# Row loads of the experts and input-tile loads issued from GpSimd's queue

## The chip, the cores and the metric

The kernel runs on one core of a Trainium2 chip. The metric is the device time of one execution in microseconds (us). Before the change it is 1392.5 us (median of 3 runs, 1391.55 to 1395.13).

A core has TensorE (PE in the profile, its weight loads PEld), VectorE (DVE), ScalarE (ACT), GpSimd (POOL) and SyncE (SP). Each executes its own instructions in order. A load between device memory and the core's own memory is issued by an instruction of SP, ACT or POOL (SPq, ACTq, POOLq in the profile, where POOL's part of the work also shows on POOL itself) and is carried out by 16 DMA engines that all queues share. Semaphores tell when it has landed.

## The reference

One decoder layer over 1024 tokens of 1024 numbers, in f32:

```python
h = rms_norm(x, attn_norm_g);  x = x + parallel_mixer(h, ...)          # two attentions, gated
h = rms_norm(x, mem_x_norm_g); x = x + memory_cross_attention(h, mem)  # 256 memory rows
h = rms_norm(x, moe_norm_g);   x = x + hierarchical_moe(h, ...)
# in the mixer: proj = h @ w_in; keys and queries are normalised and rotated (rope) by position
# in the moe:   each token picks one of 4 groups, then 2 of its 4 experts; 16 experts in all
y = y + combine[..., e] * ((silu(h @ w_gate[e]) * (h @ w_up[e])) @ w_down[e])
```

Each expert has three f32 matrices, gate and up of 1024x256 and down of 256x1024.

## The kernel before, in words

Products are made at nearly f32 accuracy: an operand is split into a high and a low part (ACT copies to the high part, DVE or POOL subtracts), and three matmuls are summed (`mm3`, L530 to L532). A planner fixes the order of the instructions on each engine when the kernel is built. It takes them by the order in which the program states them and by its own estimate of when each could start; `tc.issue_after(q)` puts what follows behind instruction `q` where both are on one engine. A tile pool with `bufs=n` has n buffers in turn, and a write to a buffer waits for the last reader of what it held.

**The start (`prep`, L733).** Eight tiles of 128 tokens of `x` go through the same steps. `load_x` (L794) loads one into one of three buffers; `square_x` (L819) sums its squares on ACT; `newton` (L546 to L552) makes the reciprocal root on DVE in 12 small instructions; L830 scales the tile with the row `grow`; PE transposes it (L608) and ACT and DVE split it into `hT`; and `project` (L530 to L532) multiplies it with 360 columns of `w_in`. These columns come in four blocks of three loads each (`kraw`, L805) and are split on ACT (L839) and on DVE and POOL in turn (L840). SP issues x tile 0, block 0, block 1, tile 1, block 2, block 3, tile 2; tiles 3 to 7 are issued by POOL as buffers come free. `table_inputs` (L663) issues seven small loads on ACT's queue: positions, frequencies, `grow`, and the four gain rows `g_k`, `g_mk`, `g_q`, `g_mq`; the gains are wanted only by `tables` (L672), which writes the tables of sines and cosines to device memory (`d_tab`), from which each tile reads its part two steps later. The first ACT instruction after them is a small activation on `ident` (L821) that loads ACT's function table.

**The experts (`moe`, L1655).** Tokens have been scattered by expert into a table `d_xs` in device memory, 1032 numbers a row, by 16 indirect DMAs of POOL (L197, `route.puts`): the vector and, behind it, its weights and token number. The experts are taken in an order by their counts, read at run time from `nb` into registers of SP (`values_load`, L1669, L1848), as SP's loads of weights and rows take their addresses from these.

- `rows_in` (L1675) loads the rows of expert number k: one DMA for each 128 rows into `xg` (two buffers, `xg_[k % 2]`, L1682) and one for their tails into `emore` (L1687). Each waits for all scatters and for the last reader of the buffer. The first 128 rows of the first two experts are loaded early (`early`), before the scatter of the second half of the tokens.
- `rows_of` (`tokens`, L1692) makes the token numbers `etok` and weights `ewt` from `emore` on DVE (L1706 to L1711), transposes the rows on PE (L1718) and splits them.
- `gate_up_in` loads gate and up in two halves of two DMAs each into `gu_raw` (L1733, two buffers); `gate_up` splits them (ACT L1747, DVE L1748). `down` loads and splits the down matrix (`dn_raw`, L1756 to L1759).
- `first_small` or `first_big` and `second` do the matmuls; ACT scales the product into `ey` (L1780, four buffers), and POOL adds it to the output by token number with an accumulating indirect DMA (`result`, L1765). Each of these waits for the one before it, as both touch the output.

Iteration i of the loop over the experts states, in this order: rows of expert i+2 (`load`), half of the gate and up weights of i+1 and its tokens, the first product of i, the other half of i+1, the down matrix of i, and the second product and result of i-1. Row loads and weight loads are all on SP's queue, in this order. Large experts (two blocks of rows) and small ones (one) alternate.

Of the kernel before, what the change touches and what calls it, by code (L numbers as in the profile page):

```python
# [498 lines left out]
class Hybrid:  # L499
# [163 lines left out]
    def table_inputs(self, pool, xp):  # L663
        nc, I = self.nc, self.I
        pi = pool.tile([128, T], I32, name="pos_i")
        p = I['positions']
        nc.scalar.dma_start(pi, bass.AP(tensor=p.tensor, offset=p.offset, ap=[[1, 128], [128, T]]))
        inv = self.row('inv_freq', 0, 32, "inv", pool, nc.scalar)
        grow = self.row('attn_norm_g', 0, D, "grow", xp, nc.scalar)
        return grow, [pi, inv] + [self.row(*a, pool, nc.scalar) for a in (('dsa_k_norm_g', 0, 64, "g_k"), ('mla_k_norm_g', 64, 32, "g_mk"), ('dsa_q_norm_g', 0, 64, "g_q"), ('mla_q_norm_g', 64, 32, "g_mq"))]  # L670

    def tables(self, pool, inputs):  # L672
        nc, I = self.nc, self.I
# [58 lines left out]
    def prep(self):  # L732
        tc, nc, I = self.tc, self.nc, self.I  # L733
        V, A, G = nc.vector, nc.scalar, nc.gpsimd
# [12 lines left out]
        tk = lambda t: slice(t * 128, (t + 1) * 128)  # L747

        def chunk(cols, pool=None, dve=False):
            n = sum(b - a for a, b in cols)  # L750
            per = 512 // n
            ws = []
            for k0 in range(0, KD, per):
                srcs, o = [], 0
                for k in range(k0, k0 + per):
                    for a, b in cols:
                        srcs.append((W[k * 128:(k + 1) * 128, a:b], o))
                        o += b - a
                hi, lo = self.wpiece(srcs, o, pool=pool, dve=dve)
                for i in range(per):  # L760
                    ws.append((hi[:, i * n:(i + 1) * n], lo[:, i * n:(i + 1) * n]))
            return ws, n
# [29 lines left out]
        xt = {}  # L792

        def load_x(t):  # L794
            xt[t] = xp.tile([128, D], F32, name="xt", bufs=3)
            (nc.sync if t < 3 else nc.gpsimd).dma_start(xt[t], I['x'][0, tk(t), :])

        c3 = ExitStack()
        load_x(0)

        kcols, kraw = ((512, 640), (1152, 1224), (1480, 1640)), []
        for h, (pool, nm) in enumerate(((kp, "kvb"), (hp, "ik_hi"), (kp, "kvb"), (hp, "ik_lo"))):
            raw, o = pool.tile([128, S], F32, name=nm)[:, 0:720].rearrange("p (k n) -> p k n", k=2), 0
            for a, b in kcols:
                nc.sync.dma_start(raw[:, :, o:o + b - a], W[h * 256:h * 256 + 256, a:b].rearrange("(k p) n -> p k n", p=128))  # L805
                o += b - a
            kraw.append(raw)
            if h % 2:
                load_x(1 + h // 2)
        tp_ = c3.enter_context(tc.tile_pool(name="tb", bufs=1, side="right"))  # L810
        grow, tin = self.table_inputs(tp_, xp)
        ckv_row = self.row('mla_ckv_norm_g', 0, 128, "ckv_row", hp)
        cq_row = self.row('mla_cq_norm_g', 0, 256, "cq_row", hp)
        ms = Stats()
        ev, st2, cTs, kvb = {}, {}, {}, {}
        xj = xp.tile([128, D], BF16, name="xj", bufs=1)

# [5 lines left out]
        for i in range(T + 7):  # L823
# [4 lines left out]
            if i < T:  # L828
                xn = xp.tile([128, D], F32, name="xn", bufs=2)
                last_xn = V.scalar_tensor_tensor(xn, xt[i], y[:, 0:1], grow, op0=OP.mult, op1=OP.mult)  # L830
                rows_T = self.transpose_rows(xn, hT[0][:, :, tk(i)], hT[1][:, :, tk(i)])
                if 2 < i + 2 < T:
                    load_x(i + 2)
            if i == 0:
                ws, n = [], 360
# [12 lines left out]
            t = i - 1  # L848
# [9 lines left out]
            t = i - 3  # L858
            if 0 <= t < T:
# [20 lines left out]
                p = self.tp()  # L880
# [9 lines left out]
            t = i - 4  # L890
# [12 lines left out]
            t = i - 6  # L903
# [15 lines left out]
        ws, n = chunk([(640, 1152)], dve=True)  # L919
        off, o = {}, 0  # L920
# [7 lines left out]
        for i in range(2, T + 2):  # L928
            if i < T:
                ev[i] = project(ws, n, i)  # L930
            t = i - 1
# [12 lines left out]
            t = i - 2  # L944
# [32 lines left out]
        ms = self.sm.tile([128, 17], F32, name="ms")  # L977
# [9 lines left out]
        for cols, o in (((1224, 1480), 0), ((0, 512), 256)):  # L987
            ws, n = chunk([cols], (self.wraw, up) if o == 0 else None)
            for t in range(T):

                at = -20 + 8 * t if o == 0 else 20 + 3 * t
# [662 lines left out]
    def moe(self, route):  # L1654
        tc, nc, I = self.tc, self.nc, self.I  # L1655
        V, G, A = nc.vector, nc.gpsimd, nc.scalar
        tk = lambda t: slice(t * 128, (t + 1) * 128)
        SP = [mybir.EngineType.SP]
        c = ExitStack()


# [4 lines left out]
        rt = route.rt  # L1666
        r1.tile([128, 8 * T], F32, name="spare")
        nb = route.nb
        lead = [nc.values_load(nb[0:1, i:i + 1], engines=SP, min_val=0, max_val=NE - 1) for i in range(2)]  # L1669
        flat = lambda p, nm, dt=F32: p.tile([128, 2048], dt, name=nm)  # L1670
        table = self.d_xs.rearrange("(e r) f -> e r f", e=NE)

# [2 lines left out]
        def rows_in(n, ex, r, xg, early=False):  # L1675


            at = slice(ex, ex + 1) if isinstance(ex, int) else ds(ex, 1)
            loads = []
            for b in range(0, n, 128):  # L1680
                m = min(128, n - b)
                last_load = nc.sync.dma_start(xg[0:m, b // 128], table[at, r + b:r + b + m, 0:D].rearrange("o p f -> (o p) f"))  # L1682
                loads.append(last_load)
            more = rt.tile([128, 2, 4], F32, name="emore", bufs=4)
            for b in range(0, n, 128):
                m = min(128, n - b)
                loads.append(nc.sync.dma_start(more[0:m, b // 128], table[at, r + b:r + b + m, D:D + 4].rearrange("o p f -> (o p) f")))  # L1687
            for q in loads:
                for p in route.puts:
                    if early and p in route.late:  # L1690
                        tc.declare_no_dep(q.ins, p.ins, reason="rows of a later block")
                    else:  # L1692
                        tc.add_manual_dep(q.ins, p.ins.name, mybir.DependencyInfo(mybir.DependencyClass.Sync, mybir.DependencyReason.DATA), reason="rows of the table")
            return n, xg, more, last_load
# [73 lines left out]
        ends, count = [None] * 4, [0]  # L1768
# [55 lines left out]
        xg3 = lambda t: t.rearrange("p (b f) -> p b f", f=D)  # L1824

        def early(i, ex, exf):

            a = (r3 if i else ra).tile([128, D], F32, name="ey" if i else "dn_raw", bufs=2)
            h, l = (eT[i][0][:, z * 1024:z * 1024 + 1024] for z in range(2))
            return rows_of(rows_in(128, ex, 0, xg3(a), True), exf, [cut(w, 128) for w in (h, l)], True)  # L1830
# [6 lines left out]
        xg_ = [flat(r1, f"xg{i}") for i in range(2)]  # L1837

        expert, loaded = [0, lead[0], lead[1]], {}

        def load(k):
            if k < NE:
                n, r = (ROOM[k] - 128, 128) if k < 2 else (ROOM[ORDER_[k]], 0)
                if k > 2:
                    with tc.issue_after(loaded[k - 1][3].ins):
                        expert.append(nc.values_load(nb[0:1, 16 + ORDER_[k]:17 + ORDER_[k]], engines=SP, min_val=0, max_val=NE - 1))  # L1848
                loaded[k] = rows_in(n, expert[k], r, xg3(xg_[k % 2]))

        def tokens(k):
            n, exf = loaded[k][0], (0.0, route.le[:, 0:1])[k] if k < 2 else route.ex[:, ORDER_[k]:ORDER_[k] + 1]
            return n, rows_of(loaded[k], exf, [cut(w, n) for w in eT[k % 2]])
# [4 lines left out]
        nb = route.places(r3)  # L1858
        raws = [gate_up_in(2, expert[2], h) for h in range(2)]
        load(0)  # L1860
        load(1)
        nA, h = tokens(0)
        last = (128, rest(), dn, *hA[2:])
        rest = first_small(128, gu1, hB)
        second(*last)
        hA = h
        load(2)
        nB, h = tokens(1)
        last = (128, rest(), dn1, *hB[2:])
# [6 lines left out]
        n, hT = tokens(2)  # L1876
# [4 lines left out]
        for i in range(2, NE):  # L1881
# [10 lines left out]
            if i + 1 < NE:  # L1892
                n, hT = n1, hT1
# [4 lines left out]
        with ExitStack() as c:  # L1898
# [5 lines left out]
            with tc.If(nov > 0):  # L1904
# [7 lines left out]
                for a, b, room in runs:  # L1912
                    r = room // 128
                    with tc.For_i(a, b, 1) as s_:
                        ne = nc.values_load(nb[0:1, ds(s_ + 32, 1)], min_val=0, max_val=9 - r)
                        ex = nc.values_load(nb[0:1, ds(s_ + 16, 1)], min_val=0, max_val=NE - 1)
                        with tc.For_i(0, ne, 1) as k:
                            ix, it, iw = op.tile([128, 1], I32, name="oix"), op.tile([128, 1], I32, name="oit"), op.tile([128, 1], F32, name="oiw")
                            at, f, num = op.tile([128, 2], F32, name="oat"), op.tile([128, 4], F32, name="of"), route.cnt[:, ds(ex, 1)]
# [18 lines left out]
                            for h in range(2):  # L1938
                                p = self.tp().rearrange("p (a b) -> p a b", a=4)
# [56 lines left out]
```

## Time and profile before

| | |
|---|---|
| median of 3 runs | 1392.5 us |
| profiled execution, whole | 1393.33 us |
| its span (first to last instruction) | 1391.6 us |
| PE busy | 1237.9 us |
| DVE, ACT, POOL busy | 949.3, 806.8, 440.1 us |
| read from and written to device memory | 134.61 and 69.70 MB |

The start is the stretch from 0 to about 60 us; the experts are from about 1085 us to the end. A group of rows of the timeline has the start in us, the duration in us, the engine, the line and operation, and in brackets the idle time before with what ended it. A window's row has its length, then the busy us of PE, PEld, DVE, ACT and POOL with their counts, the granted TensorE clock as a share of full speed, the busy share of the DMA engines and their rate in GB/s.

### The profile page before, as it was taken

Reading aid. Unit: us, or ns where it says so; the run is one execution under the profiler, and the core shown is the slowest. Engines: PE = TensorE matmul, PEld = TensorE weight load, DVE = VectorE, ACT = ScalarE, POOL = GpSimd, SP = SyncE. Lnnn points to the kernel's source line nnn. Section 1 sums busy time; section 2 is a strip of 40 time slices with the busy share of each in tenths; the row PEclk is TensorE's granted clock in tenths of the full one; section 3 lists DMA queues with packets and bytes.
Section 4 is the critical chain, followed back from the end, with each engine's and each line's share of the span. In section 5 each row is a group of like instructions: output and inputs, shape, how many; then the busy total and the mean of one; then the engine's idle time right before and its main releaser. Section 6 shows DMA issues by size and latency. Waiting matters only on the chain.

```text
span 1391.6 us, 20751 instructions
## 1 busy us (share of the span) xinstructions
PE 1237.9 (89%) x6884; PEld 1036.9 (75%) x6885; DVE 949.3 (68%) x1967; ACT 806.8 (58%) x1667; POOL 440.1 (32%) x537
## 2 busy tenths in 40 slices
PE   3998999998899999999988999999999378999983
PEld 2877778777687788887777787887888266887772
DVE  6886956799999477878977466133367735677661
ACT  4654656887662488889988322034365335676652
POOL 4565100648774322121343221121133431021111
PEclk9999999999899999999999999998999689999997
DMA  7565003543426545445221233531022757899972
GB/s 207 159 199 148 12 24 101 163 131 123 136 102 188 153 130 182 142 166 166 63 84 46 80 127 121 199 86 39 31 77 76 282 216 233 271 342 295 289 224 37
DMA packets 145557, 203.54 MB, mean 146 GB/s; under 512 B 69632, under 2 KB 90880, under 8 KB 145440
## 3 DMA queue, kind: packets, MB, share of 16 engines
q1 hardware_dynamic: 134944, 172.57, 38.4%
q0 software_dynamic: 7440, 24.71, 6.6%
q10 hardware_dynamic: 3056, 4.84, 0.9%
q8 instruction: 56, 0.92, 0.3%
q14 instruction: 61, 0.50, 0.1%
HBM read 134.61 MB, written 69.70 MB: 147 GB/s over the span
## 4 chain that ended last, share of the span: by engine, by line
PE 48%; DVE 19%; ACT 12%; DMA 11%; issue 6%; POOL 2%; SPq 1%; DVEq 0%; ACTq 0%; POOLq 0%
PE acc L530 5%; PE acc L531 5%; PE acc L532 5%; PE s L530 4%; PE s L531 4%; PE s L532 4%; DMA gu_raw<-in_moe_w_gate_dram 2%; ACT tk_junka L1222 2%; PE tp L1378 2%; PE s L955 2%; DVE ik_hi L1212 1%; PE tp L1475 1%; DVE ik_lo L1212 1%; PE acc L1392 1%; PE acc L1391 1%
## 5 line engine op out<-in xcount | busy, mean ns | idle before, releaser
L522 POOL TENSOR_TENSOR wl<-wr,wh 128x512 fp32r<-128x512 f32 (+1 forms) x78 | 102.2, 1328 | 164.1 <-ACT wh L521 120.4
L517 DVE TENSOR_TENSOR PT_lo<-tp,PT_hi 128x512 fp32r<-128x512 f32 x152 | 101.7, 685 | 28.2 <-ACT PT_hi L516 27.1
L530 PE MATMUL s<-hT_hi,wh 128*128 128x512 f32 x256 | 103.2, 403 | 3.8 <-ACT s L1083 3.8
L1765 POOL DMA_INDIRECT out_dram<-ey,etok x24 | 39.9, 1661 | 205.7 <-ACT ey L1780 42.9
L532 PE MATMUL s<-hT_hi,wl 128*128 128x512 f32 x256 | 102.3, 402 | 1.6 <-POOL wl L522 1.6
L531 PE MATMUL s<-hT_lo,wh 128*128 128x512 f32 x256 | 102.0, 401 | 0.0
L1748 DVE TENSOR_TENSOR gu_lo<-gu_raw,gu_hi 128x1024 fp32r<-128x1024 f32 x60 | 71.9, 1221 | 40.4 <-ACT gu_hi L1747 40.1
L516 ACT ACTIVATE PT_hi<-tp 128x512 fp32r<-128x512 f32 x152 | 86.8, 594 | 21.5 <-PE tp L1475 9.6
L1222 ACT ACTIVATE tk_junka<-sc,tk_b 128x512 bf16<-128x512 f32 (+2 forms) x96 | 79.4, 827 | 28.0 <-DVE tk_b L1219 27.0
L1747 ACT ACTIVATE gu_hi<-gu_raw 128x1024 fp32r<-128x1024 f32 x60 | 62.2, 1056 | 47.5 <-DMA gu_raw<-in_moe_w_gate_dram 21.6
L521 ACT ACTIVATE wh<-wr 128x512 fp32r<-128x512 f32 (+1 forms) x78 | 47.0, 619 | 73.2 <-PE acc L532 27.8
L532 PE MATMUL acc<-wh,hT_lo 128*128 128x512 f32 (+2 forms) x240 | 85.4, 356 | 0.3 <-DVE hT_lo L517 0.3
L530 PE MATMUL acc<-wh,hT_hi 128*128 128x512 f32 (+2 forms) x240 | 85.2, 356 | 0.2 <-ACT hT_hi L516 0.2
L531 PE MATMUL acc<-wl,hT_hi 128*128 128x512 f32 (+2 forms) x240 | 84.2, 352 | 0.0
L1360 DVE TENSOR_REDUCE low<-s 128x1 f32<-128x256 f32 (+3 forms) x64 | 49.1, 769 | 33.1 <-PE s L1359 32.9
L530 PEld LDWEIGHTS s<-hT_hi,wh 128*128 128x128 f32 x256 | 49.9, 195 | 14.3 <-ACT s L1083 4.5
L530 PE MATMUL s<-eT1h,gu_hi 128*128 128x224 f32 (+2 forms) x192 | 54.1, 282 | 6.9 <-DVE ewt L1711 3.6
L532 PEld LDWEIGHTS s<-hT_hi,wl 128*128 128x128 f32 x256 | 49.7, 194 | 12.0 <-POOL wl L522 2.1
L964 DVE SCALAR_TENSOR_TENSOR sc<-rel,iw,sc 128x384 f32<-128x384 f32 (+5 forms) x42 | 43.3, 1030 | 21.2 <-ACT rel L958 18.0
L531 PEld LDWEIGHTS s<-hT_lo,wh 128*128 128x128 f32 x256 | 49.7, 194 | 10.2
L530 PE MATMUL acc<-wh,mg_hi 128*128 128x512 f32 x128 | 52.4, 415 | 3.1 <-issue 3.1
L531 PE MATMUL s<-eT1l,gu_hi 128*128 128x224 f32 (+2 forms) x192 | 54.5, 284 | 0.0
(552 smaller groups left out, 4140.4 us busy)
## 6 DMA issues: line engine op xcount, KB each, us to landing
d_xs<-zero SPq DMA_DIRECT2D x32, 516.0 KB, 3.6
dn_raw<-in_moe_w_down_dram SPq DMA_DIRECT2D x32, 512.0 KB, 8.5
gu_raw<-in_moe_w_gate_dram SPq DMA_DIRECT2D x30, 512.0 KB, 7.1
gu_raw<-in_moe_w_up_dram SPq DMA_DIRECT2D x30, 512.0 KB, 8.0
wr<-in_w_in_dram SPq DMA_DIRECT2D x48, 256.0 KB, 3.1
d_g<-s SPq DMA_DIRECT2D x32, 256.0 KB, 2.4
gt<-d_g SPq DMA_DIRECT2D x16, 512.0 KB, 3.8
xg<-d_xs SPq DMA_DIRECT2D x13, 512.0 KB, 5.6
```

The lines of the kernel that those rows point to most:

```text
L516: q = self.nc.scalar.activation(hi, src, AF.Copy)
L517: self.nc.vector.tensor_sub(lo, src, hi.bitcast(F32))
L521: self.nc.scalar.activation(hi, src, AF.Copy)
L522: self.nc.gpsimd.tensor_sub(lo, src, hi.bitcast(F32))
L530: mm(out, a[0], b[0], start=start, stop=False)
L531: mm(out, a[0], b[1], start=False, stop=False)
L532: mm(out, a[1], b[0], start=False, stop=stop)
L964: last_sc = V.scalar_tensor_tensor(scv, rel[:, :Wd], g, scv, op0=OP.mult, op1=OP.add)
L1222: A.activation(junka[:, :(t + 1) * 128], blk(t), AF.Sign, bias=b[:, i:i + 1].bitcast(F32), accum_out=cnt[:, i:i + 1])
L1360: nc.vector.tensor_reduce(low[:, b:b + 1], sp[:, 0:nch, 0:w], AX.XY, OP.min)
L1747: A.activation(hi[:, z], raw_z, AF.Copy)
L1748: E.tensor_sub(lo[:, z], raw_z, hi[:, z].bitcast(F32))
```

## The change

At the start, the loads of x tiles 1 to 7 are issued by POOL (before: 3 to 7), tiles 1 and 2 now behind blocks 0 and 1 in the program's order, and the four gain rows are issued by POOL and not by ACT. Two small clears of `ms` are stated ahead of the loads. With the experts, all row loads but the early ones are issued by POOL; POOL reads the numbers of the experts into its own registers for that, and SP reads its numbers behind the last load of a down matrix (`ends[2]`) and not behind a row load.

```diff
-        return grow, [pi, inv] + [self.row(*a, pool, nc.scalar) for a in (('dsa_k_norm_g', ...), ...)]
+        return grow, [pi, inv] + [self.row(*a, pool, nc.gpsimd) for a in (('dsa_k_norm_g', ...), ...)]
...
-            (nc.sync if t < 3 else nc.gpsimd).dma_start(xt[t], I['x'][0, tk(t), :])
+            (nc.gpsimd if t else nc.sync).dma_start(xt[t], I['x'][0, tk(t), :])
+        ms = Stats()
+        ms(0), ms(1)
         load_x(0)
...
-            if h % 2:
-                load_x(1 + h // 2)
+            if h < 2:
+                load_x(1 + h)
...
+            Q = nc.sync if early else G
-                last_load = nc.sync.dma_start(xg[0:m, b // 128], table[...])
+                last_load = Q.dma_start(xg[0:m, b // 128], table[...])
-                loads.append(nc.sync.dma_start(more[0:m, b // 128], table[...]))
+                loads.append(Q.dma_start(more[0:m, b // 128], table[...]))
...
-        expert, loaded = [0, lead[0], lead[1]], {}
+        expert, loaded, row_of = [0, lead[0], lead[1]], {}, [0]
         def load(k):
             if k < NE:
                 n, r = ...
+                if k:
+                    with tc.issue_after(loaded[k - 1][3].ins):
+                        row_of.append(number(k - 1 if k < 3 else 16 + ORDER_[k], POOL))
                 if k > 2:
-                    with tc.issue_after(loaded[k - 1][3].ins):
-                        expert.append(nc.values_load(nb[0:1, ...], engines=SP, ...))
-                loaded[k] = rows_in(n, expert[k], r, xg3(xg_[k % 2]))
+                    with tc.issue_after(ends[2].ins):
+                        expert.append(number(16 + ORDER_[k], SP))
+                loaded[k] = rows_in(n, row_of[k], r, xg3(xg_[k % 2]))
```

## Rows read from the trace of the kernel before

**Rows 1.** The page, busy time of each engine.

```profile
PE 1237.9 (89%) x6884; PEld 1036.9 (75%) x6885; DVE 949.3 (68%) x1967; ACT 806.8 (58%) x1667; POOL 440.1 (32%) x537
```

**Rows 2.** The timeline of the first 17 us, every engine.

```profile
2.37 0.45 ACTq L512 DMA_DIRECT2D g_k<-in_dsa_k_norm_g_dram  x1
...
8.39 1.28 ACT L821 ACT_TABLE_LOAD   x1 [8.27 <-DMA g_q<-in_dsa_q_norm_g_dram]
...
10.09 1.06 ACT L819 ACTIVATE xj<-xt 128x1024 bf16<-128x1024 f32 x1
...
11.28 0.17 DVE L546 TENSOR_SCALAR ms<-ms 128x11 f32<-128x11 f32 x1 [9.49 <-ACT xj L819]
...
16.95 1.97 DVE L830 SCALAR_TENSOR_TENSOR xn<-xt,rq_y,grow 128x1024 f32<-128x1024 f32 x1
```

**Rows 3.** Waits of SP's queue, 0 to 60 us: us in total, times, longest.

```profile
SPq L805 <- DMA pos_i<-in_positions_dram: 2.7, 1, 2.7
```

**Rows 4.** Windows of the start: busy us, clock, DMA share, GB/s.

```profile
20.00:25.00 5.00, 4.95 (x19) 4.25 (x18) 5.00 (x18) 3.56 (x7) 2.56 (x3) 1.00 0.50 159
...
60.00:90.00 30.00, 28.03 (x155) 24.11 (x154) 28.11 (x86) 19.86 (x64) 17.21 (x40) 1.00 0.57 165
```

**Rows 5.** Issues of x tiles by queue: count, min/median/max ns of one.

```profile
L796 POOL DMA_DIRECT2D xt<-in_x_dram x5: 546/582/787, 19.2 to 50.0; - x5
```

**Rows 6.** SP's waits for PE from 1080 us on; its number reads, min/median/max ns.

```profile
SPq L1682 <- PE tp L1718: 71.2, 15, 9.2
...
L1848 SPq TENSOR_LOAD <-nb x13: 264/269/484, 1138.1 to 1299.6; - x13
```

**Rows 7.** SP's queue with the experts, timeline.

```profile
1131.02 0.34 SPq L1682 DMA_DIRECT2D xg<-d_xs  x1
...
1159.02 0.35 SPq L1682 DMA_DIRECT2D xg<-d_xs  x1
...
1160.16 0.33 SPq L1733 DMA_DIRECT2D gu_raw<-in_moe_w_gate_dram  x1
...
1197.34 7.73 SPq L1682 DMA_DIRECT2D xg<-d_xs  x2
```

**Rows 8.** ACT's splits of gate and up weights, timeline.

```profile
1148.70 2.00 ACT L1747 ACTIVATE gu_hi<-gu_raw 128x1024 fp32r<-128x1024 f32 x2
...
1167.41 1.06 ACT L1747 ACTIVATE gu_hi<-gu_raw 128x1024 fp32r<-128x1024 f32 x1 [3.35 <-DMA gu_raw<-in_moe_w_gate_dram]
```

**Rows 9.** Windows of the experts, and the sum of eleven from 1140 to 1360.

```profile
1176.00:1180.00 4.00, 3.21 (x16) 3.04 (x16) 2.75 (x7) 1.39 (x3) 1.08 (x1) 0.50 0.86 247
...
1200.00:1204.00 4.00, 4.00 (x22) 3.08 (x21) 4.00 (x6) 3.91 (x6) 0.00 (x0) 1.00 0.34 138
...
sum 220.00, PE 203.10 PEld 169.72 DVE 142.65 ACT 136.13 POOL 34.09; mean PE 18.46 PEld 15.43 DVE 12.97 ACT 12.38 POOL 3.10
```

**Rows 10.** Results of the experts: issues and landing, then three of them.

```profile
out_dram<-ey,etok POOLq DMA_INDIRECT x24, 8.1
...
1206.43 1.55 POOL L1765 DMA_INDIRECT out_dram<-ey,etok  x1 [14.75 <-DVE dn_lo L1759]
...
1361.46 1.56 POOL L1765 DMA_INDIRECT out_dram<-ey,etok  x1 [9.26 <-ACT ey L1780]
...
1379.26 1.43 POOL L1765 DMA_INDIRECT out_dram<-ey,etok  x1 [4.72 <-DMA out_dram<-ey,etok]
```

**Rows 11.** Lead-in of the experts, timeline of DVE, POOL and PE.

```profile
1107.56 4.63 DVE L1748 TENSOR_TENSOR gu_lo<-gu_raw,gu_hi 128x1024 fp32r<-128x1024 f32 x4
...
1110.04 1.85 POOL L197 DMA_INDIRECT d_xs<-xres,ix  x1 [0.31 <-issue]
...
1113.65 0.95 POOL L197 DMA_INDIRECT d_xs<-xres,ix  x1 [0.30 <-issue]
...
1132.78 2.34 POOL L1759 TENSOR_TENSOR dn_lo<-dn_raw,dn_hi 128x1024 fp32r<-128x1024 f32 x1 [8.64 <-ACT dn_hi L1758]
...
1135.15 1.94 PE L1718 MATMUL tp<-ident,xg 128*128 128x128 f32 x8 [7.34 <-DMA emore<-d_xs]
```

More of the change, by code (lines that the diff above doesn't have):

```diff
@@ L669, in table_inputs @@
         grow = self.row('attn_norm_g', 0, D, "grow", xp, nc.scalar)
-        return grow, [pi, inv] + [self.row(*a, pool, nc.scalar) for a in (('dsa_k_norm_g', 0, 64, "g_k"), ('mla_k_norm_g', 64, 32, "g_mk"), ('dsa_q_norm_g', 0, 64, "g_q"), ('mla_q_norm_g', 64, 32, "g_mq"))]
+        return grow, [pi, inv] + [self.row(*a, pool, nc.gpsimd) for a in (('dsa_k_norm_g', 0, 64, "g_k"), ('mla_k_norm_g', 64, 32, "g_mk"), ('dsa_q_norm_g', 0, 64, "g_q"), ('mla_q_norm_g', 64, 32, "g_mq"))]
     def tables(self, pool, inputs):
@@ L813, in prep @@
         cq_row = self.row('mla_cq_norm_g', 0, 256, "cq_row", hp)
-        ms = Stats()
         ev, st2, cTs, kvb = {}, {}, {}, {}
@@ L1657, in moe @@
         tk = lambda t: slice(t * 128, (t + 1) * 128)
-        SP = [mybir.EngineType.SP]
+        SP, POOL = [mybir.EngineType.SP], [mybir.EngineType.Pool]
         c = ExitStack()
@@ L1668, in moe, with number @@
         nb = route.nb
-        lead = [nc.values_load(nb[0:1, i:i + 1], engines=SP, min_val=0, max_val=NE - 1) for i in range(2)]
+        def number(at, engines):
+            return nc.values_load(nb[0:1, at:at + 1], engines=engines, min_val=0, max_val=NE - 1)
+        lead = [number(i, SP) for i in range(2)]
         flat = lambda p, nm, dt=F32: p.tile([128, 2048], dt, name=nm)
@@ L1681, in rows_in @@
                 m = min(128, n - b)
-                last_load = nc.sync.dma_start(xg[0:m, b // 128], table[at, r + b:r + b + m, 0:D].rearrange("o p f -> (o p) f"))
+                last_load = Q.dma_start(xg[0:m, b // 128], table[at, r + b:r + b + m, 0:D].rearrange("o p f -> (o p) f"))
                 loads.append(last_load)
@@ L1686, in rows_in @@
                 m = min(128, n - b)
-                loads.append(nc.sync.dma_start(more[0:m, b // 128], table[at, r + b:r + b + m, D:D + 4].rearrange("o p f -> (o p) f")))
+                loads.append(Q.dma_start(more[0:m, b // 128], table[at, r + b:r + b + m, D:D + 4].rearrange("o p f -> (o p) f")))
             for q in loads:
@@ L1845, in load @@
                 n, r = (ROOM[k] - 128, 128) if k < 2 else (ROOM[ORDER_[k]], 0)
+                if k:
+                    with tc.issue_after(loaded[k - 1][3].ins):
+                        row_of.append(number(k - 1 if k < 3 else 16 + ORDER_[k], POOL))
                 if k > 2:
-                    with tc.issue_after(loaded[k - 1][3].ins):
-                        expert.append(nc.values_load(nb[0:1, 16 + ORDER_[k]:17 + ORDER_[k]], engines=SP, min_val=0, max_val=NE - 1))
-                loaded[k] = rows_in(n, expert[k], r, xg3(xg_[k % 2]))
+                    with tc.issue_after(ends[2].ins):
+                        expert.append(number(16 + ORDER_[k], SP))
+                loaded[k] = rows_in(n, row_of[k], r, xg3(xg_[k % 2]))
         def tokens(k):
```

## The prediction

> **What bounds the kernel now.** I read the page first. PE is busy for 1237.9 of 1391.6 us [rows 1], so a change of queues can only give back time in which PE stands still or runs at its slow clock. The windows show three such places that touch the changed lines: the first 20 us, the lead-in of the experts around 1110 to 1135 us, and small gaps among the experts. For each I then read the timeline and the waits.
>
> *The start.* ACT's function table is loaded at 8.39 us, after 8.27 us of idle time, and the squares of x tile 0 follow at 10.09 [rows 2]. No tile holds them up. ACT is in order, and the issues of the gain rows stand ahead of the table load: `g_k` is issued at 2.37, and the three behind it take until 8.3. The reader should see why a small load takes so long to issue: SP shows the same, its next block of `w_in` waits 2.7 us for the landing of the positions [rows 3]. Eight loads had gone out on the two queues by 2.8 us, and each further one waits for an earlier one to land. DVE begins the root at 11.28, when the squares are there, and scales tile 0 at 16.95 [rows 2]. From then on DVE is the bound: it is busy for 5.00 of 5 us between 20 and 25 [rows 4]. From 60 us on PE has 28.03 of 30 us [rows 4].
>
> *Among the experts.* Between 1140 and 1360 us PE is busy for 203.10 of 220 us [rows 9], which leaves 16.9 us. SP's queue waits for 71.2 us, in 15 pieces, at the row load L1682, until PE has transposed the rows that the buffer held [rows 6]. The weight loads stand behind it. At 1159.02 the rows go out and at 1160.16 the first gate weights [rows 7], although ACT had begun to read the last of the weight buffers at 1148.70 and was done with it 2.00 us later [rows 8]. ACT then waits 3.35 us for those weights, until 1167.41 [rows 8]; PE has a gap, and at 1176 to 1180 the granted clock is 0.50, the slow one of its two levels (1.2 GHz) [rows 9]. The pattern returns with each large expert: from 1197.34 two row loads take 7.73 us to issue [rows 7], and in 1200 to 1204 the DMA engines have only a share of 0.34 [rows 9].
>
> *The results.* One result takes 1.55 us to issue and 8.1 us to land [rows 10], and the next has to wait for that. A pair of a large and a small expert has three: 3 x (1.55 + 8.1) = 29.0 us. From the first result of a large expert at 1206.43 to that five pairs later at 1361.46 [rows 10] a pair takes 155.0 / 5 = 31.0 us. So the chain of results has only 2.0 us to spare per pair. This caps what the experts can gain.
>
> **The change part by part.**
>
> *Gain rows from ACT to POOL.* Without them ACT can load its table from about 2.4 us on, where `g_k` was issued: 1.28 us [rows 2], and with the small activation it is free at about 4.0. The squares of tile 0 then start when the tile has landed. No row shows this landing; it lies between the 4.0 us at which ACT is free and the 8.39 us of today's table load. I take 5.1, near the early end, because tile 0 is the first load issued. DVE's chain thus starts 10.09 - 5.1 = 5.0 us earlier; the bounds are 1.7 and 6.1. As DVE is full until well after 25 us and PE from 60 us on, I let the whole shift through. The cover of the gain rows themselves is wide: the tables that want them are made behind the scaling of tile 0.
>
> *Tiles 1 and 2 from SP to POOL.* POOL's issue of a tile takes 0.58 us [rows 5]; with four gain rows these are six issues, 6 x 0.58 = 3.5 us, on an engine that has no other work yet. SP's `w_in` blocks are no longer queued behind the tiles, but 1 MB of x now moves ahead of them. Both must land before project 0 has all its columns. At worst this late block eats the shift (0 us gained); at best it costs nothing. I take nothing, since `w_in` is needed only after the transposes of tile 0. Start: -5, between 0 and -6.
>
> *Rows of the experts: lead-in.* PE stands 7.34 us, to 1135.15, for the first rows behind the scatter [rows 11], which SP issued at 1131.02 [rows 7]. On POOL an issue takes 0.58 [rows 5] where SP's took 0.34 [rows 7], and the tail behind it counts too: +0.5 us. But POOL has a subtraction from 1132.78 for 2.34 us that waits for ACT [rows 11]; if the planner leaves it ahead, the rows go out at 1135.1 and not 1131.0, +4.1 us. I take +2, between 0.5 and 4.6.
>
> *Rows of the experts: the body.* SP loses its 71.2 us of waiting, and weight loads go out when their buffers are free, for the first large expert some 8 us earlier than 1160.16. The upper end is PE's whole idle time, 16.9 us, and some 3 us for two stretches at the slow clock (3.21 us of busy time at 0.50 [rows 9], half of it lost, twice). The chain of results allows less: 2.0 us for each of some six pairs, 12 us. I take half of this, -6, because a part of the gaps belongs to DVE and ACT, which split the weights in order and whose work the change leaves as it is. POOL's added work for a pair is six issues, 3.5 us, beside 34.09 us of busy time in 220 [rows 9]. SP's number reads take 0.27 us each [rows 6]; that they now stand behind a down load adds no wait, as that load precedes them anyway. POOL's reads of the same numbers are not shown by any row; SP's 0.27 us and one whole DMA issue of 0.58 us bound them, and I take the upper end, one for each expert, in POOL's idle time. In the new waits, what is queued behind a row load on POOL is the next result and the reverse; a rival below prices that.
>
> The Trainium skill speaks against gains here: "DMA: Bandwidth & Descriptors", section "Issuing engines are not separate DMA queues", says that DMAs of different engines run on the same 16 DMA engines and that spreading them saves only the issue time. By that the body would give nothing, which is the second rival's sum. The share of 0.34 while weights were wanted [rows 9] speaks for time lost in the queue and not in the engines.
>
> *Sum.* The profiled execution took 1393.33 us, 0.8 above the median. 1393.33 - 5 + 2 - 6 = 1384.3; on the median's level 1383.5. I say 1384.
>
> **The rivals.**
>
> *POOL becomes the bound (slower).* Row loads and results share POOL's queue. A row load that waits for PE holds back a result that could go; a result that waits for the landing of the one before holds back rows. Place: the chain of results between 1160 and 1370 us. It decides as soon as more than 2.0 us of POOL's issues and waits per pair fall between the landing of one result and the issue of the next. Price: six issues of 0.58 us are 3.5 us; if they slow down beside DVE as the scatter does (1.85 us at 1110.04 while DVE splits weights, 0.95 at 1113.65 [rows 11]) they are 6.8. That is 1.5 to 4.8 us over a pair's 31.0; I take 2.2, times six pairs +13: 1393.3 - 5 + 2 + 13 = 1403. For it: the chain is nearly full already. Against it: while a result lands POOL is idle, and issues placed there are free.
>
> The scatter's two durations have a rule beside them: the Trainium skill, same page, section "SWDGE vs HWDGE vs iDMA", says that loads issued from GpSimd have their descriptors written by GpSimd, which VectorE can lock out, while those of SP and ACT are immune. By this rule the price is nearer to its upper end: +29, and 1419 in all.
>
> *Only the start gains.* The DMA engines, full in most of the experts' time, deliver the weights no earlier: 1393.3 - 5 + 2 = 1390. For it: even at 1176 to 1180, around a gap of PE, their share is 0.86 [rows 9]. Against it: the share of 0.34 at 1200.
>
> *The experts gain up to the cap.* -12 there, -5 at the start, +1 in the lead-in: 1377.
>
> *The start does nothing of what it says.* x tiles and `w_in` share the DMA engines, and the last block is as late as now, so project 0 waits for it: 1393.3 + 2 - 6 = 1389.
>
> **How the numbers follow.** The forecast 0.42 (own range 1378 to 1389), POOL as the bound 0.19, only the start 0.19, the cap 0.13, no gain at the start 0.07. What a measurement of this kernel can tell from no change is about 0.3%, 4.2 us: faster is below 1388.3, slower above 1396.7. Faster: 0.42 x 0.92 + 0.13 + a quarter of 0.19 + a third of 0.07 = 0.58. Slower: nine tenths of the first rival and a little of the others, 0.19. The rest, 0.23, is no change. The range 1371 to 1403 leaves out the upper half of the first rival and a small part of the cap case, below 0.15 together.
>
> **What would show it.** Right: the table load near 2.4 us, the squares of tile 0 near 5, DVE's scaling of tile 0 near 12; no wait of SP for PE at row loads; weight loads issued soon after ACT and DVE have split the half before; PE's idle time from 1140 to 1360 down from 16.9 to about 10 us. Wrong at the start: the squares wait for tile 0 until 8 us or later, or PE waits for columns of `w_in`. Wrong among the experts: results at intervals above 31.0 us a pair, with POOL's row loads issued right after a landing, DVE waiting longer for `emore`, or the first rows issued only after POOL's subtraction. A planner that orders other stages anew would show as a shift between 60 and 1085 us that neither end explains; I have not priced it.

## The result and the profile after

The changed kernel takes 1407.48 us (median of 4 runs, 1405.74 to 1408.61), the kernel before on the same chip 1393.82 (4 runs). The ratio is 1.0092, 95% interval [1.0067, 1.0117]: slower by 0.9%, where 1384 was forecast. The profiled run took 1405.74 us, its span is 1404.0 against 1391.6.

The page after, busy time of each engine (answers [rows 1]): the work is the same but for POOL's 50 loads.

```profile
PE 1239.1 (88%) x6884; PEld 1036.1 (74%) x6885; DVE 950.8 (68%) x1967; ACT 807.0 (57%) x1667; POOL 468.9 (33%) x587
```

The timeline of the first 17 us after (start, us, engine; answers [rows 2]):

```profile
2.50 1.28 ACT L822 ACT_TABLE_LOAD   x1 [2.37 <-issue]
...
2.96 0.54 POOL L512 DMA_DIRECT2D g_k<-in_dsa_k_norm_g_dram  x1
...
4.88 1.06 ACT L820 ACTIVATE xj<-xt 128x1024 bf16<-128x1024 f32 x1 [0.78 <-DMA xt<-in_x_dram]
...
6.06 0.17 DVE L546 TENSOR_SCALAR ms<-ms 128x11 f32<-128x11 f32 x1 [4.15 <-ACT xj L820]
...
10.22 1.28 DVE L831 SCALAR_TENSOR_TENSOR xn<-xt,rq_y,grow 128x1024 f32<-128x1024 f32 x1 [1.74 <-DMA grow<-in_attn_norm_g_dram]
```

ACT's table load comes at 2.50 in place of 8.39, the squares of tile 0 at 4.88 in place of 10.09. The first scatter of rows (L197) starts at 1077.94 us, 5.2 earlier than before. So all of the loss, 18 us, arises behind it. The lead-in on POOL, and three results (answers [rows 10, 11]):

```profile
1126.11 0.67 POOL L1688 DMA_DIRECT2D xg<-d_xs  x1 [7.18 <-DMA d_xs<-xres,ix]
...
1129.67 2.36 POOL L1765 TENSOR_TENSOR dn_lo<-dn_raw,dn_hi 128x1024 fp32r<-128x1024 f32 x1
...
1203.91 1.67 POOL L1771 DMA_INDIRECT out_dram<-ey,etok  x1 [4.06 <-ACT ey L1786]
...
1369.54 1.56 POOL L1771 DMA_INDIRECT out_dram<-ey,etok  x1 [15.62 <-ACT ey L1786]
...
1386.93 1.43 POOL L1771 DMA_INDIRECT out_dram<-ey,etok  x1 [4.77 <-DMA out_dram<-ey,etok]
```

The rows go out ahead of POOL's subtraction, not behind it. Five pairs of experts take 1369.54 - 1203.91 = 165.6 us where [rows 10] had 155.0. Most results wait for ACT, which makes `ey`. From the last issue to the end of the span pass 17.1 us; they were 12.3.

The next view shows what SP waits for after (us in total, times, longest). The wait for PE at the row loads [rows 6] is gone; a longer one, for the splits that free the weight buffers, has its place:

```profile
SPq L1739 <- DVE gu_lo L1754: 113.0, 14, 25.9
```

PE's waits and ACT's waits after, between 1140 and 1390 us:

```profile
PE acc L530 <- ACT aT_hi L516: 18.0, 5, 4.6
```

```profile
ACT gu_hi L1753 <- DMA gu_raw<-in_moe_w_gate_dram: 29.3, 10, 5.6
ACT dn_hi L1764 <- DMA dn_raw<-in_moe_w_down_dram: 18.6, 11, 3.5
```

ACT waited 21.4 and 6.0 us for these two before. Its timeline shows how that reaches PE:

```profile
1187.81 1.06 ACT L1764 ACTIVATE dn_hi<-dn_raw 128x1024 fp32r<-128x1024 f32 x1 [2.57 <-DMA dn_raw<-in_moe_w_down_dram]
1188.78 1.99 ACT L1753 ACTIVATE gu_hi<-gu_raw 128x1024 fp32r<-128x1024 f32 x2
...
1197.63 1.06 ACT L1753 ACTIVATE gu_hi<-gu_raw 128x1024 fp32r<-128x1024 f32 x1 [3.48 <-DMA gu_raw<-in_moe_w_gate_dram]
1198.59 0.37 ACT L516 ACTIVATE aT_hi<-ea 128x224 fp32r<-128x224 f32 x1
```

The planner has put the down weights of one expert ahead of the gate weights of the next, and a weight split ahead of the copy `aT_hi` that PE's second product needs. ACT is in order, stands 3.48 us for a weight, and PE stands too. PE's five waits of this kind come about one pair apart. Eleven windows from 1140 to 1360 us after sum to (answers [rows 9]):

```profile
sum 220.00, PE 195.14 PEld 163.26 DVE 137.01 ACT 132.91 POOL 57.88; mean PE 17.74 PEld 14.84 DVE 12.46 ACT 12.08 POOL 5.26
```

PE's idle time rose from 16.9 to 24.9 us, and five of these windows have a granted clock of 0.91 or less.

### The profile page after: what moved, and what is told of

Its sections match the earlier page's. It is cut to its first block, busy times and chain, and to the rows that moved or that the text cites. A ratio compares the mean times of both kernels' runs of the same rounds, so it can differ in the third digit from the quotient of the medians.

```text
span 1404.0 us, 20803 instructions
## 1 busy us (share of the span) xinstructions
PE 1239.1 (88%) x6884; PEld 1036.1 (74%) x6885; DVE 950.8 (68%) x1967; ACT 807.0 (57%) x1667; POOL 468.9 (33%) x587
## 4 chain that ended last, share of the span: by engine, by line
PE 38%; DVE 17%; DMA 12%; ACT 11%; issue 9%; POOL 3%; SPq 0%; DVEq 0%; ACTq 0%; POOLq 0%
PE acc L530 4%; PE acc L531 4%; PE acc L532 4%; DMA dn_raw<-in_moe_w_down_dram 4%; PE s L530 3%; PE s L532 3%; PE s L531 3%; DMA gu_raw<-in_moe_w_gate_dram 2%; ACT tk_junka L1223 2%; PE tp L1379 2%; DVE ik_hi L1213 2%; DVE ik_lo L1213 2%; PE s L956 1%; PE acc L1393 1%; PE acc L1392 1%
## 5 line engine op out<-in xcount | busy, mean ns | idle before, releaser
L517 DVE TENSOR_TENSOR PT_lo<-tp,PT_hi 128x512 fp32r<-128x512 f32 x152 | 101.6, 685 | 27.4 <-ACT PT_hi L516 26.2
L530 PE MATMUL acc<-dn_hi,aT_hi 128*128 128x512 f32 (+3 forms) x96 | 42.2, 440 | 20.7 <-ACT aT_hi L516 18.0
L531 PEld LDWEIGHTS s<-hT_lo,wh 128*128 128x128 f32 x256 | 49.5, 193 | 10.2
L1765 DVE TENSOR_TENSOR dn_lo<-dn_raw,dn_hi 128x1024 fp32r<-128x1024 f32 x28 | 34.1, 1225 | 31.4 <-ACT dn_hi L1764 30.6
```

The source lines that it names most:

```text
L517: self.nc.vector.tensor_sub(lo, src, hi.bitcast(F32))
L530: mm(out, a[0], b[0], start=start, stop=False)
L531: mm(out, a[0], b[1], start=False, stop=False)
```

## The experiments

Below, R1 to R24 are the starts of the 24 results in the profiled run. Theory A: the weights, no longer behind the rows, are planned so that ACT holds PE up. Theory B: GpSimd's queue is the bound. Each time is the median, with its ratio to the kernel before on the same chip.

**The parts alone.** e1 is the new `prep` and `table_inputs` with the old `moe`; e2 the reverse.

> Only the start of the change (rows on GpSimd's queue, input tiles 1 to 7 there too, split tables); the experts load their rows on SP as before. Theory A (the change loses in the experts, because loads that no longer wait on SP let the weight splits be queued on ACT ahead of copies that TensorE needs): the gain of 5.2 us that stood at the first scatter is kept to the end, 1388 to 1389 us against 1393.8 before (ratio 0.996). Theory B (GpSimd's queue of row loads and results is the bound in the experts): the same number, since GpSimd's queue is as before there. Theory C (the new order of loads at the start costs something that shows only at the end, as in the tail after the last result, 12.3 us before and 17.1 after): no gain, 1393 or more.

> Only the experts' part of the change, the start as before. Theories A and B: the two parts add, so 1407.5 + 5 = 1412 to 1413 us (ratio 1.0135). If the loss came from how the earlier start shifts the experts against each other (theory C): about as before, 1393.

e1: 1388.92 us, 0.9972 [0.9956, 0.9988]. e2: 1407.23, 1.0111 [1.0087, 1.0134], forecast 1412 to 1413. The parts add within the noise: -0.28% and +1.11%, against +0.92%. e1 is the base of what follows. Windows from R1 to R6, R6 to R15 and R15 to R24 (busy us, clock, DMA share, GB/s), e1 first, then after:

```profile
1142.52:1201.02 58.50, 53.22 (x307) 44.56 (x306) 38.07 (x79) 36.56 (x60) 7.97 (x5) 0.94 0.80 252
1201.02:1296.14 95.12, 88.95 (x584) 75.28 (x583) 64.76 (x134) 60.68 (x97) 15.84 (x9) 1.00 0.95 297
1296.14:1374.98 78.84, 64.37 (x368) 50.75 (x366) 39.53 (x62) 42.92 (x70) 13.75 (x9) 0.93 0.70 197
```

```profile
1145.04:1203.91 58.87, 52.08 (x305) 42.19 (x304) 40.65 (x80) 36.91 (x60) 15.90 (x17) 1.00 0.91 285
1203.91:1303.61 99.70, 86.50 (x538) 73.76 (x537) 61.23 (x120) 59.24 (x94) 27.16 (x27) 0.93 0.87 267
1303.61:1386.93 83.32, 71.64 (x407) 56.78 (x406) 39.43 (x72) 42.43 (x70) 16.96 (x13) 0.91 0.62 171
```

The change moves weights earlier (285 GB/s against 252 in the first stretch), wins nothing by it there, and has idle DMA engines and a slower PE later. Against e1 it loses 2.5 us up to R1, 9.4 from R1 to R24, and 4.1 after R24: 16.0, the difference of the spans. Of the 9.4, PE's idle time makes 5.7 (31.7 us against 25.9); the rest is the same matmuls taking longer (210.2 us against 206.5), at a lower granted clock in the last two stretches.

**ACT's order.** e3 queues the splits behind the copy, e6 only those from expert 5 on; e8 also puts the down splits last.

```diff
+ if m > 2:        # e6, e8: m > 4
+     o.enter_context(tc.issue_after(splits[m - 1].ins))   # last aT_hi of expert m - 3
  A.activation(hi[:, z], raw_z, AF.Copy)
...
+ with tc.issue_after(ends_gu[0].ins) if i > 2 else nullcontext():    # e8, down(): behind the splits of gate and up
      A.activation(hi, raw, AF.Copy)
```

> The whole change, and the ACT splits of the gate and up weights of expert m are queued behind the ACT split of the activations of expert m - 3, so that the copy that TensorE's next product needs no longer stands behind a weight that is late (five places, 3.5 to 5.6 us each, 18.0 us of TensorE's waits in all after the change). Theory A: 12 to 18 us come back, 1389 to 1396 us. Theory B (GpSimd's queue): nothing, 1405 to 1409. Theory D (the transfers themselves are late, since the weights go out in bursts and the down weights then take 11 to 14 us): TensorE's wait only changes its place, 1402 to 1409.

> As the run in which the copy goes first, but only for the weights of expert 5 and on, so that the lead-in and the first experts keep the order of the changed kernel. Against the run of the start alone, the changed kernel lost 2.5 us up to the first result, 0.4 to the sixth, 4.6 from the sixth to the fifteenth, 4.5 from there to the last and 4.1 after the last. Theory A (ACT's order, in the body): the sixth result at 1204, as in the changed kernel, then about 94 to 96 us to the fifteenth and 79 to 81 to the last, as in the run of the start alone; 1395 to 1400 us in all. If the 94.6 us that the other run had there were luck of its shifted start: 1403 to 1408.

> As the run with the copy first from expert 5 on (1402.2 us), and ACT's splits of the down weights of expert i are queued behind all gate and up splits of expert i + 1, more like the order before the change. Theory A, if the down weights' place in ACT's queue is the rest of the loss in the body: from the sixth result to the last about 174 us, as with the start alone, against 178.3 in that run: 1394 to 1399. If only the activation copy mattered: 1400 to 1404. If the down splits now come too late for TensorE's second product: 1405 or more.

e3: 1404.52, 1.0071 [1.0047, 1.0096]; e6: 1402.18, 1.0057 [1.0036, 1.0078]; e8: 1402.33, 1.0051 [1.0032, 1.0070]. PE's wait for the copy in e3, same stretch:

```profile
PE acc L530 <- ACT aT_hi L516: 2.0, 2, 1.3
```

The wait fell from 18.0 to 2.0 us, but by the ratios only 3 to 6 us came back (e3 2.9, e6 4.9, e8 5.7), less than theory A had forecast each time. Theory A in this form is too narrow: the copy is where much of the loss showed, not all that made it.

**Who issues the rows.** e9 keeps the rows on SP, but traces `load(i + 2)` behind `down(i)`, so no weight waits for them. e5 keeps them on POOL and makes the first gate load of an expert wait for PE's transposes of the rows before. e11 leaves the four columns of `emore` on SP, e12 the 1024 of `xg`.

```diff
-     load(i + 2)                             # e9
  dn = down(i, expert[i], V)
+     load(i + 2)
...
+ if m > 2 and h == 0:                        # e5, gate_up_in()
+     tc.add_manual_dep(q.ins, ends_tp[0].ins.name, ...)
...
- loads.append(Q.dma_start(more[0:m, b // 128], table[at, ...]))       # e11; e12: the same for xg
+ loads.append(nc.sync.dma_start(more[0:m, b // 128], table[at2, ...]))
```

> The start of the change; the rows of expert i + 2 stay on SP but are put behind the weights of experts i + 1 and i, so that no weight waits behind them and GpSimd's queue is as before. ACT's queue comes out nearly in the order of the changed kernel (down weights ahead of gate and up weights, a weight split ahead of the second activation copy). Theory A: the body loses 5 to 9 us as in the changed kernel although GpSimd has nothing to do with it, 1393 to 1400; TensorE waits for ACT's copy about 3 to 5 us in each pair. Theory B (GpSimd's queue is what costs): 1386 to 1390. If the row load's wait on SP had held the body back before: below 1386.

> The whole change with rows on GpSimd's queue, but the first gate and up loads of expert m wait on SP for the transposes of expert m - 1's rows, as the row load in front of them did before the change. GpSimd's queue does what it does after the change. Theory A and theory D: the weights go out at the old times and ACT's queue has about the old order, so the experts take what they took before or a little less: 1385 to 1391 us. Theory B: GpSimd's queue is still the bound, 1403 to 1409.

> The whole change, but of the row loads only the 1024 columns of the token vectors are on GpSimd's queue, the four columns with the weights and numbers stay on SP. ACT's order is that of the changed kernel. Theory A: the body as in the changed kernel (about 99 us from the sixth to the fifteenth result), 1402 to 1408 with the longer end, 1398 to 1404 without it. Theory B (GpSimd's queue with its loads): half of its loads are gone, 1395 to 1400. The end after the last result: 17 us if any row load on GpSimd's queue brings it, 13 if not.

> The other half: the 1024 columns on SP as before, so that the weights wait behind them as before; the four columns (a load as dear to issue) on GpSimd's queue, behind the register reads. ACT's order is close to that of the start alone. Theory A: the body takes what it takes with the start alone (93 to 96 us from the sixth to the fifteenth result), 1387 to 1391, or 4 more with the longer end. Theory B: half of the added work of GpSimd, so half of the loss in the body, 1394 to 1400. The end after the last result: 17 us if any row load there brings it.

e9: 1401.06, 1.0041 [1.0024, 1.0058]; e5: 1419.91, 1.0197 [1.0171, 1.0224]; e11: 1401.94, 1.0050 [1.0032, 1.0067]; e12: 1408.31, 1.0105 [1.0075, 1.0136]. e9 is the telling one: GpSimd's queue is as before, and the whole kernel still loses about 10 us against e1 (1.0041 against 0.9972). Its R1 to R24 takes 245.9 us (e1 232.5, after 241.9), but its profiled run is the longest of seven, 5.9 us above the median, so the size of that loss is uncertain. Here is R6 to R15:

```profile
1209.76:1312.78 103.02, 86.77 (x532) 73.78 (x531) 60.91 (x120) 59.37 (x94) 15.74 (x10) 0.90 0.86 257
```

Between 1140 and 1390 us ACT waits 28.6 us for gate and 23.1 for down weights, about as in after. PE does not wait 3 to 5 us in each pair for the copy `aT_hi`, as expected (3.5 us once), but for another copy on ACT, that of the rows:

```profile
PE s L530 <- ACT eT1h L516: 11.6, 5, 3.9
```

e11's body, with half of the loads on POOL, is that of after: 241.2 us. Yet by the whole times e11 is about 6 us faster than after; the end explains 2.0 of them (below), and its profiled run, the longest of six, does not show the rest. So a part for POOL's queue is not excluded.

e5 and e12 were forecast wrong. There the rows on POOL come behind results that wait for ACT, and DVE waits for them; e5, then e12 (before the change it was 13.6 us in ten waits):

```profile
DVE etok L1714 <- DMA emore<-d_xs: 26.8, 6, 11.9
```

```profile
DVE etok L1713 <- DMA emore<-d_xs: 19.3, 7, 9.6
```

So theory B's mechanism exists. The changed kernel does not meet it in this form: DVE waits there 8.0 us for `emore`. e8 does (33.5 us), which may be why its better order on ACT gave back no more.

**More bytes.** e10 is e1 with a copy of 256 KB for each expert on SP, from DRAM to DRAM.

```diff
  dn = down(i, expert[i], V)
+ nc.sync.dma_start(spare[i % 2], I['moe_w_down'][0, i].rearrange("(p q) d -> p (q d)", q=4)[:, 0:1024])
```

> The start of the change, and for each expert from the third on SP also copies 256 KB of the down weights to a spare place in DRAM, which nobody reads: only the DMA engines have more to do. With the start alone the stretch from the sixth to the fifteenth result moved 297 GB/s at a DMA share of 0.95, with TensorE busy 0.94 of it. If the transfers are at their limit there: 0.25 MB by 297 GB/s is 0.9 us for each of six experts, 4 to 7 us more in that stretch and 8 to 13 in all, 1397 to 1402. If TensorE is the only bound: 0 to 2 us in all, 1389 to 1391. (ACT's order comes out a little different.)

e10: 1400.62, 1.0044 [1.0025, 1.0062], in the range of transfers at their limit. R6 to R15 takes 98.8 us (e1 95.1). But DMA's share there is 0.90, PE is busy for 93.17 us, and the clock is 0.95; ACT's order changed as well. And of the 9.4 us by which its span exceeds e1's, 4.9 lie ahead of the first scatter, where nothing had been copied. It does not settle how much of this is bytes.

**A third buffer.** `gu_raw` holds the two halves of gate and up, `dn_raw` two of down. h1 is after with a third `gu_raw`, h2 e1 with it, both with two `ey` in place of four; h3 and h4 have a third `dn_raw` and three `ey`.

```diff
- raw = r2.tile([128, 2, 4, 256], F32, name="gu_raw", bufs=2)
+ raw = r2.tile([128, 2, 4, 256], F32, name="gu_raw", bufs=3)
```

> The changed kernel with a third buffer for the gate and up weights (room for it from the result buffers: two in all in place of four). If the buffers hold the body since the change (SP waits 113 us for gate and up splits): 5 to 9 us of the body come back, 1397 to 1402 us, and SP's wait on the splits falls below half. If not: 1404 to 1409. If the fewer result buffers cost: above 1409.

> The start alone, rows on SP, with the same third gate-and-up buffer and two result buffers. There TensorE is busy 0.94 and the transfers 0.95 of the stretch from the sixth to the fifteenth result, so a buffer more gives nothing: 1386 to 1392. If buffers were a bound already before: 1380 to 1385.

> The changed kernel with a third buffer for the down weights (three result buffers in place of four). ACT's order in the body stays that of the changed kernel, with the late split ahead of TensorE's copy. If the buffers are the bound: 1399 to 1403. If the order on ACT and the late gate weights are: 1404 to 1409.

> The start alone, rows on SP, with the third down buffer and three result buffers: nothing to be won by the same reason as with the third gate-and-up buffer, 1386 to 1392; 1380 to 1385 if the buffers were a bound before.

h1: 1398.99, 1.0051 [1.0033, 1.0069]; h2: 1401.85, 1.0063 [1.0045, 1.0081]; h3: 1422.73, 1.0216 [1.0192, 1.0240]; h4: 1413.74, 1.0154 [1.0127, 1.0182]. The three stretches of h1, and ACT's wait:

```profile
1148.38:1205.99 57.61, 51.97 (x300) 43.05 (x299) 41.62 (x82) 38.60 (x61) 17.66 (x18) 0.97 0.92 294
1205.99:1299.72 93.73, 85.36 (x540) 71.33 (x540) 61.99 (x120) 59.43 (x94) 24.97 (x27) 0.96 0.91 283
1299.72:1373.30 73.58, 66.48 (x411) 53.19 (x409) 38.10 (x71) 40.90 (x69) 15.76 (x13) 0.99 0.64 181
```

```profile
ACT gu_hi L1753 <- DMA gu_raw<-in_moe_w_gate_dram: 10.6, 5, 4.4
```

R1 to R24 takes 224.9 us: 17.0 less than after and 7.6 less than e1, with all loads and results still on POOL. SP's wait for the splits fell only to 79.5 us, not below half as expected; what fell to a third is ACT's wait for gate weights. The profiled run (1392.46) is the shortest of seven, 6.5 us under its median: for the whole kernel the gain over after is 8.5 us by the medians and 5.7 by the ratios, no more than e8's. A third down buffer gives nothing in the body (h3 241.0, h4 232.4); both runs lose 19 and 22 us before R1, which I did not follow. h2 lost where nothing was expected: there ACT waits 15.4 us for results to land before it can write `ey`. But i2 below waits 13.3 us in the same way and has a shorter body, so why h2 lost is not shown, nor what the buffer alone does with the old order.

**Does that buffer need GpSimd?** i1 is h1 with the first three row loads on SP, i2 is e9 with the third `gu_raw` and two `ey`.

```diff
- Q = nc.sync if early else G
+ Q = nc.sync if early or on_sp else G       # i1: on_sp = k < 3
```

> The changed kernel with the third gate-and-up buffer, and the first three row loads (the lead-in) back on SP. Body 225 to 234 us from the first to the last result, the end 16.5 to 17 us after the last result's issue (38 row loads left on GpSimd's queue in place of 44), the first result 1 to 4 us earlier than the 1148.4 of the run with the third buffer: 1389 to 1397 us in all. If the lead-in's loss was not the row loads on GpSimd's queue but the early weights: the first result still at 1147 to 1149, 1397 to 1400.

> The start of the change, rows on SP behind the weights, with the third gate-and-up buffer. If it is only SP's wait and the buffers: the body as with GpSimd's queue and the third buffer, 225 to 234 us against 245.9 of the same order with two buffers, and the short end of 13 us: 1385 to 1394. If the rows need their own queue: 1398 or more.

i1: 1400.75, 1.0057 [1.0032, 1.0081]; i2: 1399.18, 1.0040 [1.0020, 1.0059]. From R6 to R24: after 183.0 us, e9 182.3; with the buffer h1 167.3, i1 168.5, i2 170.0. In these single executions the queue matters little and the buffer 12 to 16 us. The whole times do not bear this out on SP: i2 (1.0040) is no faster than e9 (1.0041), for e9's profiled run is the longest of seven and i2's the second shortest of twelve. i2's 1399.18 also lies where its expectation put "the rows need their own queue". So the buffer's gain stands for h1 alone, and whether it needs the rows on their own queue is not shown. i1's R1 came at 1146.3, and from R1 to R6 it lost 7.0 us against e1. All three stay behind e1: what they win in the body they lose in the lead-in (R1 at 1146 to 1148) or after R24, and by their medians they win less than in the profiled run.

**The end.** e7a is e1 with the numbers also read into POOL's registers, e7b e1 with 132 one-column writes on POOL.

```diff
+ nc.values_load(nb[0:1, at:at + 1], engines=[mybir.EngineType.Pool], ...)   # e7a, in load(k)
...
+ for _ in range(132):                                                       # e7b
+     G.memset(tiny, 0.0)
```

> The start of the change, rows on SP, and the expert numbers read into GpSimd's registers as well, at the places where the change reads them, and not used. It asks where the 4.1 us after the last result come from (17.1 us from the last result's issue to the end of the span in the changed kernel, 13.0 with the start alone). If the register reads are their cause: 17 here; if not: 13. The body of the experts: nothing, or up to 2 us if the reads hold the results up.

> The start of the change, rows on SP, and 132 writes of one column on GpSimd's queue before the experts' body: GpSimd executes about as many more instructions as with the change. If the number of instructions on GpSimd's queue makes the end later (loading of code at the end): 17 us from the last result's issue to the end of the span; if not: 13. The stage itself may come some us later if the writes stand in front of a weight split.

One run each: 1390.37 and 1389.03 us; from R24 to the end 13.0 and 13.3. Neither is the cause. SP's last wait, for PE's sequencer at the end of the program, in e1, e11 and after:

```profile
SPq L1992 <- PEq L1992: 5.0, 2, 4.5
```

```profile
SPq L2001 <- PEq L2001: 6.9, 2, 6.3
```

```profile
SPq L2000 <- PEq L2000: 8.7, 2, 8.1
```

Its longest piece follows the count of loads that a run has moved to POOL's queue, those of the start included: before 4.0 us, 6 (e1) 4.5, 28 (e11, e12) 6.3, 44 (e2, i1) 7.6, 50 (after) 8.1. That is (8.1 - 4.0) / 50 = 0.08 us each, and 3.6 of the 4.1 us that after loses against e1 behind R24.

## Why the prediction failed, by its steps

*Start, -5: right at the squares, smaller behind them.* The squares of tile 0 start 5.2 us earlier, near the forecast 5.0. But the prediction let the whole shift through, and at the scaling of the last tile 1.8 us of it are left (before, then after):

```profile
69.28 2.17 DVE L830 SCALAR_TENSOR_TENSOR xn<-xt,rq_y,grow 128x1024 f32<-128x1024 f32 x1
```

```profile
67.44 2.17 DVE L831 SCALAR_TENSOR_TENSOR xn<-xt,rq_y,grow 128x1024 f32<-128x1024 f32 x1
```

That the first scatter shows 5.2 us again is in part luck: in profiled runs with the new start it comes between 1075.6 (e7b) and 1083.3 us (h4), before at 1083.1. The firm figure is e1's ratio, 3.9 us less. That tiles 1 and 2 cost nothing is in accord with this, but no run moved them alone.

*Lead-in, +2: hardly there.* The first transposes come no later than in e1 (1130.56 against 1130.87), the second half of the first `ey` 0.2 us later (1141.72 against 1141.55). The rows were not put behind POOL's subtraction. R1 itself comes 2.5 us later than in e1, because row loads for a later expert stand ahead of it on POOL's queue (e1, then after):

```profile
1142.52 1.66 POOL L1766 DMA_INDIRECT out_dram<-ey,etok  x1 [12.19 <-ACT ey L1781]
```

```profile
1142.42 1.12 POOL L1688 DMA_DIRECT2D xg<-d_xs  x2 [8.48 <-PE tp L1724]
1143.62 1.12 POOL L1693 DMA_DIRECT2D emore<-d_xs  x2
1145.04 2.68 POOL L1771 DMA_INDIRECT out_dram<-ey,etok  x1 [0.30 <-ACT gu_hi L1753]
```

So the marker R1 shows POOL's queue there, a late result and not late work of PE, and the loss in the body is nearer to 11.7 us than to 9.4. e9's R1 is late for another reason: its first scatter came 3.6 us later than e1's. In h1, h2, i1 and i2 the second half of the first `ey` comes 65.8 to 67.6 us after the first scatter, and 63.1 to 64.4 in all others but h3 and h4. So a later lead-in goes with the third buffer (or the fewer `ey`), whichever queue issues the rows.

*Body, -6: the step that failed.* It counted SP's 71.2 us of waiting as something to win, and took ACT's and DVE's work as left as it is. The weight loads did go out earlier, the first of the body by 14.5 us (e1, then after):

```profile
1155.10 0.33 SPq L1734 DMA_DIRECT2D gu_raw<-in_moe_w_gate_dram  x1
```

```profile
1140.63 0.34 SPq L1739 DMA_DIRECT2D gu_raw<-in_moe_w_gate_dram  x1
```

Nothing was won by it. The wait of SP moved to the splits (113.0 us), the planner moved the splits ahead on ACT, ACT's wait for gate and down weights rose from 27.4 to 47.9 us, and the body lost 9.4 us from R1 to R24, where 6 were to be won. e9 shows a loss without GpSimd. What made it is shown only in part: e8, by ACT's order, and h1, by a third gate-and-up buffer, each bring the ratio from 1.0092 to 1.0051, and ACT's wait for gate and down weights to 10.2 and 18.3 us. No run has both, and about half of the loss in the body stays without a shown cause. A second fault is in the upper end. The 16.9 us of PE's idle time were one sum over unlike stretches. Between R6 and R15 the kernel with the old order has PE busy for 88.95 of 95.12 us at a clock of 1.00 and the DMA engines at 0.95, so nothing much was to be won there; the idle time lies at both ends of the body.

The Trainium skill's rule ("DMA: Bandwidth & Descriptors", "Issuing engines are not separate DMA queues"), by which the body would give nothing, agrees with the traces: with the same buffers, and no weights queued behind rows, it makes little difference which engine issues the rows (by their ratios h1 1.0051, i2 1.0040). It does not give the loss.

*POOL's added work, hidden: nearly right.* The rival with POOL as the bound named 1403, near the result; its mechanism holds back results such as R1, but no run shows it as the main loss. Here are all row loads after on POOL (min/median/max ns):

```profile
L1688 POOL DMA_DIRECT2D xg<-d_xs x22: 522/588/1200, 1126.1 to 1322.0; - x22
L1693 POOL DMA_DIRECT2D emore<-d_xs x22: 518/552/1146, 1126.8 to 1322.7; - x22
```

The eight `xg` loads that took 1.1 to 1.2 us are those that start while a result before them is still being issued; the others took 0.52 to 0.67. So the slow issues here go with a result just ahead; that VectorE slows them, as the rival's upper price assumed, is not shown. The six issues of one pair (1246.99 to 1262.65) come to 5.1 us, with overlaps, inside the rival's 3.5 to 6.8. Nor did the chain of results set the cap it was given: h1's two pairs from R15 to R21 take 28.2 us each, below 29.0.

*Not priced: the end, +4.1, and the planner.* I had looked for its new orders between 60 and 1085 us; they came among the experts.

What stays open: why e3, e6 and e8, with PE's extra waits mostly gone, still have PE busy for 3 to 7 us more than e1 between R1 and R24. The granted clock is 0.90 to 0.98 in their later stretches where e1 has 1.00 and 0.93, and no run shows what alone would hold it up. Also open are the later lead-in with the third buffer, and why each load on POOL's queue makes the end longer.

## What to carry to other kernels

When a queue waits, look at what would be late next before counting the wait as gain: here the weights that ACT has to split. Ask whether a stretch has room at all, by PE's busy time, clock and DMA share in that stretch and not over the stage. A planner answers a load that it believes early with a new order on in-order engines, so a moved load has to be judged with the order that comes of it. Of this change the start alone is worth keeping: e1, 0.9972 [0.9956, 0.9988], beats both kernels.

## What the runs showed of the hardware

Loads on GpSimd's queue made the end of the program longer by 0.08 us each, whatever their size (22 loads of 4 columns as much as 22 of 1024: 6.3 us both); 132 small writes or the register reads did not (4.5 us). An issue on GpSimd took 0.54 us for a gain row at the start and 0.59 us (median) for an `xg` load among the experts, but 1.1 to 1.2 us right behind a result; SP's issue of an `xg` load took 0.34 us (median, e1).
